# A two-layer FoX and GLA trunk: the sums of squares of three norms added up ahead of the product with ones

## The chip, the cores and the metric

The kernel runs on one core of one Trainium2 chip. The metric is the device time of one execution in microseconds (us), median of several runs. TensorE is called PE here, its weight loads PEld; VectorE is DVE, ScalarE ACT, GpSimd POOL, and SyncE, which issues most DMAs, SP.

## The reference, cut to what matters

A sequence of 1024 tokens of width 1024 passes two layers. Each has a token mixer (forgetting attention in layer 0, gated linear attention in layer 1) and a SwiGLU, and each of the four sub-layers is preceded by an RMS norm with shift and scale:

```python
def rms_norm(x, g):
    xf = x.astype(jnp.float32)
    y = xf * lax.rsqrt(jnp.mean(xf * xf, axis=-1, keepdims=True) + EPS)
    return (y * g.astype(jnp.float32)).astype(x.dtype)
...
    h = modulate(rms_norm(x, norm1_g[i]), sh1, sc1)
...
    x = x + g1[:, None, :] * y
    h = modulate(rms_norm(x, norm2_g[i]), sh2, sc2)
    x = x + g2[:, None, :] * swiglu(h, ffn_w_in[i], ffn_w_out[i])
```

The change concerns how the sum over the 1024 channels of `xf * xf` is formed in three of these norms.

## The kernel before, in words

Activations lie transposed: channels on the 128 partitions, in eight tiles of 128 channels, tokens along the free side. Tokens are worked in two halves of 512. Matrix products are made of three float32r products of a high and a low part (`mm3`, L241 to L243), with a pace that PE sets through most of the program.

A sub-layer ends in `last_chunk`. It projects the last four blocks of the inner dimension, for the first half of the tokens and then for the second. For each of the eight channel tiles m, DVE adds the scaled product to the residual stream (`x`, L1061), ACT squares the new tile (L577), and the object `SumSq` adds squares together, on POOL or DVE (L584). What it has not added up at the end are its *roots*. `rms_cols` (L524 to L534) then sums over partitions and roots at once: for each of four blocks of 128 tokens it multiplies every root, as the stationary operand, with a column of ones, and accumulates in one column of a PSUM tile `sp` (L529). DVE adds EPS to the mean (L532, tile `rs`), POOL raises it to the power -0.5 (L533), and four products (L541, tile `rb`) spread the result over all partitions, for DVE to multiply with.

In the first half there is one root (four products). In the second half `SumSq` has `late` = 7 (`LATE1`): the eighth square is not added to anything, and of the first seven there are three sums, so that there are four roots, v[0] (tiles 0 to 3), v[4] (tiles 4 and 5), v[6] and v[7], and sixteen products. This happens in three places: **place 1**, the norm ahead of the SwiGLU of layer 0 (tile `sp011`); **place 2**, the norm ahead of the gated linear attention (`sp101`); **place 3**, the norm ahead of the SwiGLU of layer 1 (`sp111`). The last norm has another form (`late` = 0) and isn't touched.

The products with ones are covered by other work on PE: at places 1 and 3 by the first tiles of the SwiGLU (`plain_tile`, tile `p`), which work on the first half of the tokens, at place 2 by the value projection of the first tokens (`gv_body`, tile `gv`). `issue_after` puts the products behind them in the order. Otherwise a scheduler orders each engine's instructions by a timeline of its own, so an edit may move others too. Each engine takes its instructions in that order.

At place 2 the two buffer slots named s39 and s40 hold four of the squares (v[3], v[4], v[5], v[7]). They are used next for the tiles `ad` (the running sum and two raw tiles of the second layer's modulation, and the mask that a DVE memset at L1567 fills). SP loads the raw tiles (L361), ACT scales them (L375, L377), POOL adds them (L379).

At places 1 and 3 POOL makes the sums of weight blocks (`op_sums`, L702 to L704) when their raw tiles `xv` have landed.

## Time and profile before

| | |
|---|---|
| median of 3 runs | 2429.87 us (2428.5 to 2430.59) |
| profiled execution, its own time | 2430.71 us |
| its span, first to last instruction | 2429.0 us |
| PE busy | 2375.2 us, 98% |
| DVE, ACT, POOL busy | 1689.5, 1192.6, 1164.0 us |
| mean granted clock of TensorE | 0.992 |

Times in a timeline are microseconds from the start of the span. A row gives the start, how long the instructions last, engine, line, operation, the tile written and those read, shapes, how many instructions are merged in the row, and in brackets how long the engine sat idle just before and what ended that. A float32 product appears as two passes (x2) of a weight load and a matmul. A matmul's end is modelled, and matmuls overlap, so the time that one takes from PE is read from the start of one to the start of the next. A table by windows gives for each stretch the engines' busy time, and the clock that TensorE was granted (1.00 is full speed).

### The profile page before, as it was taken

How to read it: one execution, taken by the hardware profiler on the slowest of the kernel's cores; microseconds unless marked ns; L12 is line 12 of the kernel's file. 1: busy time of each engine (PE TensorE's matmuls, PEld its weight loads, DVE VectorE, ACT ScalarE, POOL GpSimd, SP SyncE). 2: the span in 40 equal slices, each digit the busy share in tenths (PEclk: the TensorE clock that was granted, in tenths of full speed). 3: DMA queues.
4: the chain of work that ended last, by engine and by line, in shares of the span. 5: the costliest groups of instructions: out<-in, count | busy, mean ns of one | idle time of the engine just before them, and what ended most of it. 6: DMA issues, size and time to landing. Idle time of an engine off the chain costs nothing.

```text
span 2429.0 us, 36104 instructions
## 1 busy us (share of the span) xinstructions
PE 2375.2 (98%) x12338; PEld 2019.5 (83%) x12338; DVE 1689.5 (70%) x2845; ACT 1192.6 (49%) x2286; POOL 1164.0 (48%) x1015
## 2 busy tenths in 40 slices
PE   7999999999999999999999999999999999999998
PEld 6788888878888888888888798898888888888888
DVE  6578777676687777766788545436587767666787
ACT  4656556666544444445324756654343334345325
POOL 3333333333337878753363544552335656653362
PEclk9999999999999999999999999999999999999999
DMA  9233333123326555457665334444325434347664
GB/s 271 80 105 113 94 108 113 62 88 120 118 96 192 180 167 171 156 187 262 229 204 168 83 114 117 126 126 156 109 84 186 152 135 155 128 169 258 231 209 148
DMA packets 329503, 362.40 MB, mean 149 GB/s; under 512 B 24476, under 2 KB 252984, under 8 KB 329320
## 3 DMA queue, kind: packets, MB, share of 16 engines
q1 hardware_dynamic: 329128, 360.09, 46.2%
q8 instruction: 97, 1.59, 0.3%
q14 instruction: 86, 0.70, 0.1%
q10 hardware_dynamic: 192, 0.02, 0.0%
HBM read 269.78 MB, written 90.24 MB: 148 GB/s over the span
## 4 chain that ended last, share of the span: by engine, by line
PE 78%; DVE 6%; DMA 6%; ACT 3%; issue 2%; POOL 2%; SPq 2%; DVEq 0%; POOLq 0%; ACTq 0%
PE p_b L241 16%; PE p_b L243 16%; PE p_b L242 16%; PE o_b L968 2%; PE t_b L954 2%; SPq L361 1%; DMA ad_s<-in_ada_w_dram 1%; PE qk_b L241 1%; PE qk_b L242 1%; PE qk_b L243 1%; DMA ada_s<-in_ada_w_dram 1%; PE s_b L923 1%; PE s_b L924 1%; PE vps_b L241 1%; PE vps_b L242 1%
## 5 line engine op out<-in xcount | busy, mean ns | idle before, releaser
L164 DVE TENSOR_TENSOR o_s<-xv_s,o_s 128x512 fp32r<-128x512 f32 (+1 forms) x376 | 333.4, 890 | 82.3 <-ACT o_s L163 81.3
L163 ACT CAST o_s<-xv_s 128x512 fp32r<-128x512 f32 (+1 forms) x376 | 217.9, 586 | 319.5 <-PE p_b L243 250.8
L934 POOL TENSOR_SCALAR lp_s<-lp_s,st 128x128 f32<-128x128 f32 (+7 forms) x128 | 98.5, 775 | 291.1 <-DVE st L933 273.1
L242 PE MATMUL p_b<-B,o_s 128*128 128x512 f32 x608 | 237.8, 391 | 0.0
L243 PE MATMUL p_b<-B,o_s 128*128 128x512 f32 x608 | 237.2, 391 | 0.0
L241 PE MATMUL p_b<-B,o_s 128*128 128x512 f32 x608 | 236.6, 392 | 0.0
L702 POOL TENSOR_TENSOR ex_s<-xv_s,xv_s 128x512 f32<-128x512 f32 (+1 forms) x64 | 86.4, 1350 | 270.2 <-DMA xv_s<-in_ffn_w_in_dram 108.3
L241 PE MATMUL p_b<-T,o_s 128*128 128x512 f32 x480 | 186.7, 389 | 0.0
L242 PE MATMUL p_b<-T,o_s 128*128 128x512 f32 x480 | 186.7, 389 | 0.0
L243 PE MATMUL p_b<-T,o_s 128*128 128x512 f32 x480 | 180.7, 389 | 0.0
L932 ACT ACTIVATE lp_s<-lp_s,st 128x128 f32<-128x128 f32 (+7 forms) x128 | 99.3, 776 | 76.7 <-DVE st L928 73.9
L241 PEld LDWEIGHTS p_b<-B,o_s 128*128 128x128 f32 x608 | 115.0, 189 | 23.8
L243 PEld LDWEIGHTS p_b<-B,o_s 128*128 128x128 f32 x608 | 114.7, 189 | 24.0
L242 PEld LDWEIGHTS p_b<-B,o_s 128*128 128x128 f32 x608 | 114.9, 189 | 23.7
L1306 DVE TENSOR_TENSOR ex_s<-ex_s,p_b 128x512 f32<-128x512 f32 x140 | 93.6, 680 | 31.8 <-PE p_b L243 31.7
L704 POOL TENSOR_TENSOR xv_s<-ex_s,xv_s 128x512 f32<-128x512 f32 (+1 forms) x64 | 85.9, 1342 | 52.3 <-DVE o_s L164 49.7
L163 ACT CAST pt_s<-t_b 128x512 fp32r<-128x512 f32 (+1 forms) x160 | 79.9, 548 | 62.5 <-PE t_b L954 61.6
L243 PEld LDWEIGHTS p_b<-T,o_s 128*128 128x128 f32 x480 | 90.1, 188 | 18.8
L241 PEld LDWEIGHTS p_b<-T,o_s 128*128 128x128 f32 x480 | 90.1, 188 | 18.7
L242 PEld LDWEIGHTS p_b<-T,o_s 128*128 128x128 f32 x480 | 90.1, 188 | 18.6
L164 DVE TENSOR_TENSOR pt_s<-t_b,pt_s 128x512 fp32r<-128x512 f32 (+1 forms) x160 | 96.5, 631 | 11.4 <-ACT pt_s L163 10.8
L968 PE MATMUL o_b<-pt_s,v_s 128*128 128x256 f32 x512 | 95.6, 295 | 5.9 <-DVE pt_s L164 4.2
(1950 smaller groups left out, 7494.7 us busy)
## 6 DMA issues: line engine op xcount, KB each, us to landing
xv_s<-in_ffn_w_in_dram SPq DMA_DIRECT2D x176, 256.0 KB, 3.3
hid_B<-x SPq DMA_DIRECT2D x70, 512.0 KB, 2.8
ad_s<-in_ada_w_dram SPq DMA_DIRECT2D x384, 64.0 KB, 2.0
hid_T<-x SPq DMA_DIRECT2D x36, 512.0 KB, 2.8
xv_s<-in_ffn_w_out_dram SPq DMA_DIRECT2D x96, 192.0 KB, 5.1
ada_s<-in_ada_w_dram SPq DMA_DIRECT2D x128, 128.0 KB, 2.7
xv_s<-in_ffn_w_out_dram SPq DMA_DIRECT2D x40, 256.0 KB, 2.8
T2o<-hid_T SPq DMA_DIRECT2D x18, 512.0 KB, 9.0
```

The source lines that it names most:

```text
L163: nc.scalar.copy(hi, src)
L164: nc.vector.tensor_sub(lo, src, hi.bitcast(F32))
L241: nc.tensor.matmul(ps, ah, bh, start=start, stop=False)
L242: nc.tensor.matmul(ps, ah, bl, start=False, stop=False)
L243: nc.tensor.matmul(ps, al, bh, start=False, stop=stop)
L702: nc.gpsimd.tensor_add(s1, a21, a22)
L704: nc.gpsimd.tensor_sub(a11, s1, a11)
L932: nc.scalar.activation(lp, lp, AF.Exp, bias=mcur, scale=-1.0, accum_out=st[:, qi, 2:3])
L934: nc.gpsimd.tensor_scalar(lp, lp, st[:, qi, 3:4], 1.0, op0=ALU.mult, op1=ALU.mult)
L954: nc.tensor.transpose(tp[:, i, :], lps[qi][:, psl(2 * b + jj)], ident)
L968: nc.tensor.matmul(ops, lv, pts[b][:, hl, 2 * jj:2 * jj + 2, :], start=j == 0 and hl == 0, stop=False)
L1306: nc.vector.tensor_add(d, d if src is None else dest(G, src), ps)
```

## The change

The first seven squares are added up to one sum. Two additions on DVE come right behind the square of the seventh tile: v[4] += v[6], v[0] += v[4]. The roots of the second halves are then v[0] and v[7]: eight products with ones at each of the three places.

```diff
@@ -569,8 +569,7 @@
             self.late = late
-            self.roots = {0: [self.v[0]], 8: [self.v[0]], 7: [self.v[0], self.v[4], self.v[6], self.v[7]],
-                          5: [self.v[0], self.v[4], self.v[5], self.v[6], self.v[7]]}[self.late]
+            self.roots = [self.v[0], self.v[7]] if late == 7 else [self.v[0]]
 
@@ -583,6 +582,9 @@
                 d *= 2
+            if m == 6 and self.late == 7:
+                for i, j in ((4, 6), (0, 4)):
+                    nc.vector.tensor_add(v[i], v[i], v[j])
```

Lines behind the edit are numbered two higher in the changed kernel. On PE at place 1, before, the products `sp011` follow the last product of a SwiGLU tile (`p0`). In the slots' names, ss0_s31 holds v[0], s34 v[4], s32 v[6] and s33 v[7]; the four products of the first token block end this piece (a product with v[0] for it stands 27 rows earlier, and the other blocks follow with the same four).

```order
L241 MATMUL p0_b4_1_7658<-B2103_7112,o00001_s20_2_7452 128x512
L242 MATMUL p0_b4_1_7658<-B2103_7112,o00001_s20_2_7452 128x512
L243 MATMUL p0_b4_1_7658<-B2103_7112,o00001_s20_2_7452 128x512
L529 MATMUL sp011_b6_3_7485<-ones_74,ss0_s34_7104 128x1
L529 MATMUL sp011_b6_3_7485<-ones_74,ss0_s32_7102 128x1
L529 MATMUL sp011_b6_3_7485<-ones_74,ss0_s33_7103 128x1
L529 MATMUL sp011_b6_3_7485<-ones_74,ss0_s31_7101 128x1
```

On PE at place 1, after the change, the same rows read:

```order
L241 MATMUL p0_b4_1_7652<-B2103_7112,o00001_s20_2_7452 128x512
L242 MATMUL p0_b4_1_7652<-B2103_7112,o00001_s20_2_7452 128x512
L243 MATMUL p0_b4_1_7652<-B2103_7112,o00001_s20_2_7452 128x512
L529 MATMUL sp011_b6_3_7487<-ones_74,ss0_s31_7101 128x1
L529 MATMUL sp011_b6_3_7487<-ones_74,ss0_s33_7103 128x1
```

The eight products stand where fifteen stood, the sixteenth, which stood earlier, is gone, and the first of them now reads v[0], the sum that is finished last. Places 2 and 3 look the same.

On DVE at place 1 the last rows of the second half of the projection, before, up to the step that reads `sp011`:

```order
L1061 SCALAR_TENSOR_TENSOR x0_6_6208<-fo1461p_b2_15_7455,modc_168,x0_6_6208 128x512
L1061 SCALAR_TENSOR_TENSOR x0_7_6209<-fo1471p_b3_16_7470,modc_168,x0_7_6209 128x512
L584 TENSOR_TENSOR ss0_s34_7104<-ss0_s34_7104 128x512
L532 TENSOR_SCALAR rs011_7502<-sp011_b6_3_7485 128x4
L1162 SCALAR_TENSOR_TENSOR yb0_s31_7526<-x0_0_6202,amul_169,rb011_b7_4_7505 128x512
```

The same on DVE after the change:

```order
L1063 SCALAR_TENSOR_TENSOR x0_6_6208<-fo1461p_b2_15_7455,modc_168,x0_6_6208 128x512
L1063 SCALAR_TENSOR_TENSOR x0_7_6209<-fo1471p_b3_16_7472,modc_168,x0_7_6209 128x512
L583 TENSOR_TENSOR ss0_s34_7104<-ss0_s34_7104 128x512
L587 TENSOR_TENSOR ss0_s34_7104<-ss0_s34_7104,ss0_s32_7102 128x512
L587 TENSOR_TENSOR ss0_s31_7101<-ss0_s31_7101,ss0_s34_7104 128x512
L532 TENSOR_SCALAR rs011_7496<-sp011_b6_3_7487 128x4
```

The two additions stand behind the last one that was there, and nothing else moves; place 3 looks the same. At place 2 other work stands between. On DVE, before, from the last residual tile of the SwiGLU (`x0_7`) on; se0_s40 holds v[4], s38 v[6], s36 v[0], `w2t` is a small weight, `gvt00` the split of the first value tile, `ad_s40` the mask:

```order
L1061 SCALAR_TENSOR_TENSOR x0_7_6209<-f0e11871p_b5_16_12886,modc_168,x0_7_6209 128x512
L584 TENSOR_TENSOR se0_s40_12503<-se0_s40_12503 128x512
L164 TENSOR_TENSOR w2t_12977<-w2raw_s18_93_12974,w2t_12977 16x512 x2
L164 TENSOR_TENSOR gvt00_s53_1_13074<-gv00_b0_1_13012,gvt00_s53_1_13074 128x512
L1567 MEMSET ad_s40_12966 128x512
L1568 MEMSET ad_s40_12966 128x4
L532 TENSOR_SCALAR rs101_12918<-sp101_b3_1_12901 128x4
```

On DVE at place 2 after the change:

```order
L1063 SCALAR_TENSOR_TENSOR x0_7_6209<-f0e11871p_b5_16_12882,modc_168,x0_7_6209 128x512
L583 TENSOR_TENSOR se0_s40_12497<-se0_s40_12497 128x512
L164 TENSOR_TENSOR w2t_12965<-w2raw_s18_93_12962,w2t_12965 16x512 x2
L587 TENSOR_TENSOR se0_s40_12497<-se0_s40_12497,se0_s38_12495 128x512
L164 TENSOR_TENSOR gvt00_s53_1_13062<-gv00_b0_1_13000,gvt00_s53_1_13062 128x512
L587 TENSOR_TENSOR se0_s36_12494<-se0_s36_12494,se0_s40_12497 128x512
L1569 MEMSET ad_s40_12954 128x512
L1570 MEMSET ad_s40_12954 128x4
L532 TENSOR_SCALAR rs101_12906<-sp101_b3_1_12897 128x4
```

The additions come in behind `w2t` and behind `gvt00`. ACT behind place 2, before, from the first modulation tiles (`ad`) on; `te0` and `h1` are the normed second half, `gvt01` the split of the second value tile:

```order
L375 ACTIVATE ad_s39_12965<-ad_s39_12965,cblk_97 128x512
L377 ACTIVATE ad_s40_12966<-ad_s40_12966,cblk_97 128x512
L377 ACTIVATE ad_s39_12965<-ad_s39_12965,cblk_97 128x512
L555 ACTIVATE h1h0_12676<-te0_s31_12504,modc_168 128x512
L560 ACTIVATE te0_s31_12504<-te0_s31_12504,modc_168,amul_169 128x512
L555 ACTIVATE h1h2_12680<-te0_s32_12505,modc_168 128x512
L561 CAST h1h1_12678<-te0_s31_12504 128x512
L377 ACTIVATE ad_s40_12966<-ad_s40_12966,cblk_97 128x512
L163 CAST gvt01_s25_2_13134<-gv01_b1_2_13077 128x512
```

ACT there after the change:

```order
L377 ACTIVATE ad_s40_12954<-ad_s40_12954,cblk_97 128x512
L375 ACTIVATE ad_s39_12953<-ad_s39_12953,cblk_97 128x512
L555 ACTIVATE h1h0_12670<-te0_s31_12498,modc_168 128x512
L377 ACTIVATE ad_s39_12953<-ad_s39_12953,cblk_97 128x512
L560 ACTIVATE te0_s31_12498<-te0_s31_12498,modc_168,amul_169 128x512
L555 ACTIVATE h1h2_12674<-te0_s32_12499,modc_168 128x512
L163 CAST gvt01_s25_2_13122<-gv01_b1_2_13065 128x512
```

The cast of `gvt01` stands two rows earlier, ahead of a cast and of an `ad` tile, and `h1h0` comes ahead of the third `ad` tile. SP issues the four DMAs of the first `ad_s40` tile ahead of those of `ad_s39`, where two of each alternated. On PE one product `z` of the gate stands three `gv` products later.

## Prediction

> **What bounds the kernel now.** I read the page first, then the chain of work that ended last, then the timelines of the three places, and a table of windows for the granted clock. The page says where the time is:

> ```profile
> span 2429.0 us, 36104 instructions
> PE 2375.2 (98%) x12338; PEld 2019.5 (83%) x12338; DVE 1689.5 (70%) x2845; ACT 1192.6 (49%) x2286; POOL 1164.0 (48%) x1015
> ```

> PE is busy for 98% of the span, so what PE is spared counts, and what PE must newly wait for counts as well. The chain that ended last holds the products with ones at all three places:

> ```profile
> 676.42 3.50 PE sp_b L529 x30
> ...
> 1327.35 3.08 PE sp_b L529 x26
> ...
> 1772.05 3.45 PE sp_b L529 x30
> ```

> They are on the path, about 3.5 us at each place. Place 1 on PE, as a timeline:

> ```profile
> 669.66 0.28 PE L529 MATMUL sp_b<-ones,ss_s 128*128 128x1 f32 x2
> ...
> 676.03 0.39 PE L243 MATMUL p_b<-B,o_s 128*128 128x512 f32 x1
> 676.26 3.66 PE L529 MATMUL sp_b<-ones,ss_s 128*128 128x1 f32 x30
> 679.77 0.77 PE L241 MATMUL p_b<-B,o_s 128*128 128x512 f32 x1
> ...
> 683.72 0.40 PE L243 MATMUL p_b<-B,o_s 128*128 128x512 f32 x1
> 683.95 1.06 PE L541 MATMUL rb_b<-ident,rs 128*128 128x128 f32 x8
> ```

> Three things are to be seen. Fifteen products take 30 passes from 676.26 to 679.77, 0.117 us a pass, 0.23 us a product; the sixteenth stands alone at 669.66 and costs as much. A product of the SwiGLU starts 0.23 us behind the one before. And the twelve such products from 679.77 to 683.95 took 4.18 us where 12 x 0.23 is 2.7. The table by windows says why, and shows the same elsewhere (the windows are the stretches in which the clock records change, all 3.41 us long and on one grid through the whole trace):

> ```profile
> 675.83:679.25 3.42, 3.42 (x31) 1.00 0.45 178
> 679.25:682.66 3.41, 3.41 (x11) 0.50 0.03 7
> 1324.37:1327.78 3.41, 2.73 (x24) 1.00 1.00 300
> 1327.78:1331.19 3.41, 3.41 (x32) 1.00 0.80 265
> 1331.19:1334.61 3.42, 3.42 (x19) 0.50 0.67 179
> 1341.43:1344.85 3.42, 1.31 (x6) 1.00 0.35 88
> 1344.85:1348.26 3.41, 3.41 (x8) 0.50 0.30 73
> 1771.51:1774.93 3.42, 3.42 (x31) 1.00 0.46 183
> 1774.93:1778.34 3.41, 3.41 (x11) 0.50 0.00 0
> ```

> The third column is the granted clock. After a window filled with products of one column, and after one in which PE mostly waited (1.31 us busy of 3.42), the clock is 0.50 for a window. Eight products started in such a window (1344.85), 0.43 us each, where 15 would have: about 1.5 us lost. A window with a wait of 0.7 us in it (1324.37) had no such effect. I call PE **thinly used** when it waits or makes one-column products; somewhere between 1.3 and 2.27 us of that in one window halves the next one. I take 2.1 us, near the rows that did halve.

> **What the change removes.** Eight products with ones at each place, 16 passes of 0.117 us: 1.87 us on PE, 5.6 us for the three. That would be the gain, 0.23%, if nothing waited.

> **What it adds: two additions on DVE ahead of the first product.** The products are in order on PE, and the first of them now needs v[0], finished last. Behind it waits all of PE. So the question is when the two additions end. At place 1, DVE and POOL:

> ```profile
> 674.48 0.68 DVE L584 TENSOR_TENSOR ss_s<-ss_s 128x512 f32<-128x512 f32 x1
> ```

> ```profile
> 674.70 1.61 POOL L702 TENSOR_TENSOR ex_s<-xv_s,xv_s 128x512 f32<-128x512 f32 x1 [14.24 <-DMA xv_s<-in_ffn_w_in_dram]
> 676.39 1.27 POOL L703 TENSOR_TENSOR xv_s<-xv_s 128x512 f32<-128x512 f32 x1
> ```

> The last addition that exists ends at 675.16, and DVE is then free. Two more at 0.68 us each, with 0.05 us between them, would end at 676.6. But POOL's addition at 674.70 takes 1.61 us where the next takes 1.27: it waited for DVE's. That the two engines take turns, and DVE waits as well, is shown by the first half at place 3, where DVE's additions last 1.16 and 1.11 us beside one on POOL:

> ```profile
> 1742.92 1.16 DVE L584 TENSOR_TENSOR ss_s<-ss_s 128x512 f32<-128x512 f32 x1
> 1744.11 1.11 DVE L584 TENSOR_TENSOR ss_s<-ss_s,ss_s 128x512 f32<-128x512 f32 x1
> ```

> ```profile
> 1743.49 1.19 POOL L209 TENSOR_TENSOR wo_768l_s<-wo_s,wo_768h_s 128x256 fp32r<-128x256 f32 x1
> ```

> POOL's ends at 1744.68, 0.6 us behind the end of DVE's first (1744.08), and DVE's second ends at 1745.22, 0.55 us behind POOL's. So at place 1 I let them take turns: POOL's L702 ends at 676.31 as now; the first new addition ends 0.55 us later, 676.86; POOL's L703, pending since 676.39, ends 1.15 us behind that (as L702 does behind 675.16), 678.01; the second new addition ends at 678.56. PE, 0.23 us ahead without the early product, comes to the products at 676.03 and waits till 678.6. Sixteen passes take 1.87 us, to 680.5, against 679.77 now: **0.7 us later**. Thin use lasts from 676.03 to 680.5, 4.5 us, and so one half-clock window follows as now; where a window's edge lies early in the stretch (I put it at one run in three), a second follows, 1.6 us more.

> Place 3 has the same work, with POOL's additions a little later:

> ```profile
> 1770.11 0.68 DVE L584 TENSOR_TENSOR ss_s<-ss_s 128x512 f32<-128x512 f32 x1
> ```

> ```profile
> 1771.06 1.28 POOL L702 TENSOR_TENSOR ex_s<-xv_s,xv_s 128x512 f32<-128x512 f32 x1 [14.98 <-DMA xv_s<-in_ffn_w_in_dram]
> ```

> ```profile
> 1771.89 3.61 PE L529 MATMUL sp_b<-ones,ss_s 128*128 128x1 f32 x30
> 1775.36 0.77 PE L241 MATMUL p_b<-B,o_s 128*128 128x512 f32 x1
> ```

> The first new addition runs from 1770.84 to 1771.52 and is ahead of POOL; POOL's follows, to 1772.67; the second ends at 1773.22. Products from 1773.28 to 1775.15, against 1775.36: **0.2 us earlier**. Thin use lasts 3.5 us, as now.

> At place 2 POOL is idle, but DVE isn't. DVE, then PE:

> ```profile
> 1326.62 0.67 DVE L584 TENSOR_TENSOR se_s<-se_s 128x512 f32<-128x512 f32 x1
> 1327.22 1.38 DVE L164 TENSOR_TENSOR w2t<-w2raw_s,w2t 16x512 fp32r<-16x512 f32 x2
> 1328.63 0.69 DVE L164 TENSOR_TENSOR gvt_s<-gv_b,gvt_s 128x512 fp32r<-128x512 f32 x1
> ...
> 1344.11 0.69 DVE L164 TENSOR_TENSOR gvt_s<-gv_b,gvt_s 128x512 fp32r<-128x512 f32 x1 [0.85 <-ACT gvt_s L163]
> ```

> ```profile
> 1327.35 3.51 PE L529 MATMUL sp_b<-ones,se_s 128*128 128x1 f32 x30 [0.68 <-DVE se_s L584]
> 1330.72 0.36 PE L241 MATMUL gv_b<-wv_0h_s,h1h 128*128 128x256 f32 x1
> ...
> 1335.16 1.05 PE L541 MATMUL rb_b<-ident,rs 128*128 128x128 f32 x8
> ...
> 1342.35 0.39 PE L1592 MATMUL aps_b<-h1l,aw_s 128*128 128x512 f32 x1
> 1344.85 0.79 PE L241 MATMUL gr_b<-h1h,w_h_s 128*128 128x512 f32 x1 [2.11 <-DVE gvt_s L164]
> ```

> PE already waits here for v[4] (0.68 us). By the new order DVE does both `w2t` splits (to 1328.60), an addition (to 1329.2), `gvt00` (to 1329.9) and the second addition, to 1330.5. The products then run from 1330.55 to 1332.4, against 1330.72: 1.7 us later, and `rb` with them, 1.5 us more if a second half-clock window follows, which is likelier here (thin use for 5.9 us). But behind `rb` PE has 7.4 us of work (1335.16 to 1342.58) and then waits 2.27 us for `gvt01`. That wait gets shorter: the cast of `gvt01` stands two rows earlier on ACT, DVE waited 0.85 us for it, and so `gr` follows `rb` by 8.85 us, not 9.7. PE waits 1.4 us there in place of 2.27, under what halves the clock, and the half window from 1344.85 (1.6 us) goes. `gr` ends 1.7 - 0.85 - 1.6 = 0.8 us earlier, or with the second window 0.7 us later. I take **nothing** for place 2.

> The additions' own time on DVE, 6 x 0.68 us, lies where DVE was idle (4.8 us at places 1 and 3 ahead of L532). Moved `ad` DMAs start some 2 us later, but the running sum is due only after 1364. Nothing else moves.

> **The sum.** 0.7 + 0 - 0.2 = 0.5 us more. On the profiled execution, 2430.71 us with 1.7 us around its span, this gives 2431.2; it ran 0.84 us above the median, so for a median I say 2430.4 us.

> **The rivals.** *The turns are missed*, because a DMA of `xv` lands later and POOL comes behind both additions. Then the products start at 676.7 and 1772.3, end 1.2 us earlier than now at both places: -2.4 us in all. If thin use (2.7 us) then halves no clock there, 1.45 us more at each: -5.3, 2424.5 us. For it: landing times vary (POOL came 0.22 us behind DVE's start at place 1, 0.95 at place 3). Against: POOL must come 1 us later at place 1. One in twelve.

> *The clock stays full at places 1 and 3* though the turns are as I say: 0.7 - 1.45 and -0.2 - 1.45, -2.4 us in all, 2427.5 us. Against it are the rows: 3.5 us of thin use halved it. For it: the place's edge on the grid is by chance, and the bound of 2.1 us isn't sharp. One in six. [...]

> *The delay at place 2 is not absorbed.* The late products free v[7]'s slot late, SP's `ad` loads start after them, and ACT, in order, waits for the third `ad` tile ahead of `te0` as now, so that `gvt01` keeps its 9.7 us behind `rb`, PE its wait, and the clock its half window. Then place 2 costs 1.7 us, 3.2 with a second window; with the two windows at place 1 as well (2.3) and -0.2, 5.3 us in all: 2435.2 us, slower than before. It decides from the point where the `ad` tile lands more than 0.85 us behind `h1h0`. Against it: `h1h0` now stands ahead of that tile. One in six, half of it with only one window at place 1 or 2, some 2433.

> That the scheduler undid the edit can't be: its rows are in the order above.

> **How the numbers follow.** Forecast as above, with -1.5 to +2.8 us by windows, 0.58; turns missed 0.08; clock full 0.17; not absorbed 0.17. The range takes in the second and most of the last, less and plus 1 us by which runs differ: 2426.5 to 2434.5. A measurement can tell about 0.2%, 4.9 us, from no change. Beyond that lie, on the fast side, half of the first rival: 0.05; on the slow side half of the last: 0.09; within: 0.86.

> **What would show it.** The products with ones as 16 passes at each place; PE idle ahead of them, released by DVE's second addition, 2.6 us at place 1, 1.6 at place 3, 4 at place 2; POOL's L703 between the two additions at place 1; a shorter wait at `gr`. I am wrong if DVE makes both additions in a row beside POOL, if the clock is full behind the products, or if `gr` waits as long as before.

## The result, and the profile after

The changed kernel takes 2435.38 us (median of 20 runs, 2432.1 to 2442.91), the kernel before 2429.47 us (20 runs beside them, 2424.64 to 2430.89). The ratio is 1.0028, 95% interval 1.0022 to 1.0034: by this ratio slower by 6.8 us (5.3 to 8.3); the two medians lie 5.9 us apart. The forecast was no change, 2430.4 us, with 2434.5 us as the upper end.

The page of the changed kernel (its profiled execution took 2435.12 us):

```profile
span 2433.4 us, 36022 instructions
...
PE 2372.8 (98%) x12290; PEld 2017.9 (83%) x12290; DVE 1708.6 (70%) x2851; ACT 1196.4 (49%) x2286; POOL 1165.7 (48%) x1015
```

PE has 48 passes less (24 products), as meant. It is busy 2.4 us less, and yet the span is longer. Place 1 as a timeline, all engines, of which these rows matter:

```profile
671.13 1.86 POOL L704 TENSOR_TENSOR ex_s<-xv_s,xv_s 128x512 f32<-128x512 f32 x1 [13.99 <-DMA xv_s<-in_ffn_w_in_dram]
671.16 0.67 DVE L583 TENSOR_TENSOR ss_s<-ss_s 128x512 f32<-128x512 f32 x1
671.94 3.27 DVE L587 TENSOR_TENSOR ss_s<-ss_s,ss_s 128x512 f32<-128x512 f32 x2
673.07 1.59 POOL L705 TENSOR_TENSOR xv_s<-xv_s 128x512 f32<-128x512 f32 x1
...
675.36 3.52 PE L529 MATMUL sp_b<-ones,ss_s 128*128 128x1 f32 x16 [2.51 <-DVE ss_s L587]
678.75 0.77 PE L241 MATMUL p_b<-B,o_s 128*128 128x512 f32 x1
...
683.20 1.05 PE L541 MATMUL rb_b<-ident,rs 128*128 128x128 f32 x8
```

PE stands still for 2.51 us until DVE's second addition ends. The two additions last 3.27 us where 1.36 would do, with POOL's second one between them. Then come 16 passes, which last from 675.36 to 678.75, 3.4 us: nearly as long as the 30 passes of before (3.5 us). The windows on the clock's grid say why (columns: window, its length, PE's busy time and matmuls, granted clock, DMA share and GB/s):

```profile
671.98:675.40 3.42, 0.91 (x5) 1.00 0.61 241
675.40:678.81 3.41, 3.41 (x17) 0.50 0.00 0
678.81:682.22 3.41, 3.41 (x9) 0.50 0.01 2
682.22:685.64 3.42, 3.42 (x20) 1.00 0.02 5
```

Behind the window with the wait in it (PE busy for 0.91 us of 3.42) the next has a clock of 0.50; the products with ones run in it, 16 passes in 3.4 us, and fill it to the end; and the one behind it has 0.50 as well. Two half-clock windows, where the kernel before had one. Place 3, as a timeline:

```profile
1772.18 1.90 POOL L704 TENSOR_TENSOR ex_s<-xv_s,xv_s 128x512 f32<-128x512 f32 x1 [13.96 <-DMA xv_s<-in_ffn_w_in_dram]
1772.26 0.68 DVE L583 TENSOR_TENSOR ss_s<-ss_s 128x512 f32<-128x512 f32 x1
1773.04 3.26 DVE L587 TENSOR_TENSOR ss_s<-ss_s,ss_s 128x512 f32<-128x512 f32 x2
...
1776.44 2.22 PE L529 MATMUL sp_b<-ones,ss_s 128*128 128x1 f32 x16 [2.50 <-DVE ss_s L587]
```

The same picture: a wait of 2.50 us, and by the clock records two half windows, from 1777.9 to 1784.7. Place 2, as a timeline:

```profile
1324.30 0.67 DVE L583 TENSOR_TENSOR se_s<-se_s 128x512 f32<-128x512 f32 x1
1324.89 1.38 DVE L164 TENSOR_TENSOR w2t<-w2raw_s,w2t 16x512 fp32r<-16x512 f32 x2
1326.31 0.69 DVE L587 TENSOR_TENSOR se_s<-se_s,se_s 128x512 f32<-128x512 f32 x1
1326.92 0.68 DVE L164 TENSOR_TENSOR gvt_s<-gv_b,gvt_s 128x512 fp32r<-128x512 f32 x1
1327.52 0.68 DVE L587 TENSOR_TENSOR se_s<-se_s,se_s 128x512 f32<-128x512 f32 x1
1328.35 3.55 PE L529 MATMUL sp_b<-ones,se_s 128*128 128x1 f32 x16 [3.65 <-DVE se_s L587]
```

and its windows:

```profile
1323.93:1327.34 3.41, 0.77 (x7) 1.00 0.79 276
1327.34:1330.75 3.41, 2.40 (x12) 0.50 0.76 217
1330.75:1334.17 3.42, 3.42 (x17) 0.50 0.24 69
1334.17:1337.58 3.41, 3.41 (x18) 0.50 0.19 51
```

A wait of 3.65 us behind `w2t` and `gvt00`, and three half windows in a row. PE's waits, summed over the whole execution by the view of waits (total, number, longest), show both new ones:

```profile
PE sp_b L529 <- DVE ss_s L587: 5.0, 2, 2.5
...
PE sp_b L529 <- DVE se_s L587: 3.6, 1, 3.6
```

To see where the time went I measured the same stretches in every profiled execution: at places 1 and 3 from the first SwiGLU product (tile `p`) to `rb`, at place 2 from the first value product `gv` to the gate product `z`, all as starts on PE.

| stretch, us | before | after | difference |
|---|---|---|---|
| place 1, `p` to `rb` | 14.74 | 17.31 | +2.57 |
| place 2, `gv` to `z` | 35.50 | 37.28 | +1.78 |
| place 3, `p` to `rb` | 14.73 | 16.82 | +2.09 |

Together 6.4 us, close to the measured 6.8. The rest of the two traces does not count against the change: ahead of place 1, where the kernels are the same, after is 3.3 us earlier (before's execution had two half windows at 300 us that after's had not), and the attention of layer 1, from the first product of `kdt` to the last tile of its projection, took 377.24 us in before and 378.95 in after; but it took 378.7 to 381.0 in the five other kernels below that keep four roots at place 2, so that before's execution was the odd one.

One execution of each kernel is a small sample of half windows. The granted clock of every execution is a larger one: its mean is 0.9910 over the 20 executions of the changed kernel, and 0.9930 to 0.9932 in the four groups of executions of the kernel before that ran beside the experiments below (13 to 34 each). A half window (3.41 us at 0.50) takes 0.0007 off the mean clock of an execution of 2430 us, so by this estimate the changed kernel has some three half windows more than before, worth about 1.7 us each.

### The profile page after: what moved, and what is told of

Its sections match the earlier page's. It is cut to its first block, busy times and chain, and to the rows that moved or that the text cites. A ratio compares the mean times of both kernels' runs of the same rounds, so it can differ in the third digit from the quotient of the medians.

```text
span 2433.4 us, 36022 instructions
## 1 busy us (share of the span) xinstructions
PE 2372.8 (98%) x12290; PEld 2017.9 (83%) x12290; DVE 1708.6 (70%) x2851; ACT 1196.4 (49%) x2286; POOL 1165.7 (48%) x1015
## 5 line engine op out<-in xcount | busy, mean ns | idle before, releaser
L164 DVE TENSOR_TENSOR o_s<-xv_s,o_s 128x512 fp32r<-128x512 f32 (+1 forms) x376 | 338.4, 903 | 81.7 <-ACT o_s L163 80.7
L163 ACT CAST o_s<-xv_s 128x512 fp32r<-128x512 f32 (+1 forms) x376 | 218.9, 588 | 322.7 <-PE p_b L243 254.1
L243 PE MATMUL p_b<-B,o_s 128*128 128x512 f32 x608 | 237.6, 391 | 0.0
L241 PE MATMUL p_b<-B,o_s 128*128 128x512 f32 x608 | 237.1, 393 | 0.0
L241 PE MATMUL p_b<-T,o_s 128*128 128x512 f32 x480 | 186.7, 389 | 0.0
L243 PE MATMUL p_b<-T,o_s 128*128 128x512 f32 x480 | 180.7, 389 | 0.0
L243 PEld LDWEIGHTS p_b<-B,o_s 128*128 128x128 f32 x608 | 115.1, 189 | 24.1
L241 PEld LDWEIGHTS p_b<-B,o_s 128*128 128x128 f32 x608 | 115.1, 189 | 23.8
L163 ACT CAST pt_s<-t_b 128x512 fp32r<-128x512 f32 (+1 forms) x160 | 80.1, 549 | 62.0 <-PE t_b L956 61.1
L243 PEld LDWEIGHTS p_b<-T,o_s 128*128 128x128 f32 x480 | 90.1, 188 | 18.7
L241 PEld LDWEIGHTS p_b<-T,o_s 128*128 128x128 f32 x480 | 90.1, 188 | 18.6
L164 DVE TENSOR_TENSOR pt_s<-t_b,pt_s 128x512 fp32r<-128x512 f32 (+1 forms) x160 | 96.5, 631 | 11.4 <-ACT pt_s L163 10.9
```

The costliest lines, as they stand in the source:

```text
L163: nc.scalar.copy(hi, src)
L164: nc.vector.tensor_sub(lo, src, hi.bitcast(F32))
L241: nc.tensor.matmul(ps, ah, bh, start=start, stop=False)
L243: nc.tensor.matmul(ps, al, bh, start=False, stop=stop)
```

## The experiments

Theory A: PE's wait for the late additions is the loss, with the half-clock windows that it brings. Its rivals: the additions cost by themselves (B), place 2 alone is the loss (C), the eight products left halve the clock even without a wait (D), and later E, that POOL's additions delay other work by as much as PE is spared. Ratios are against the kernel before, run beside each; one thousandth is 2.4 us.

| run | ratio (95%) | us | place 1, 3, us | place 2, us |
|---|---|---|---|---|
| changed kernel | 1.0028 (1.0022 to 1.0034) | +6.8 | 17.31, 16.82 | 37.28 |
| e1: place 2 only | 1.0020 (1.0011 to 1.0029) | +4.9 | (14.58, 13.14) | 37.79 |
| e2: places 1 and 3 only | 1.0028 (1.0017 to 1.0040) | +6.8 | 15.69, 17.27 | (34.83) |
| e3: fewer products, no additions, two sums left out | 0.9956 (0.9944 to 0.9969) | -10.7 | 11.35, 11.35 | 30.92 |
| e4: additions, all products | 1.0002 (0.9993 to 1.0011) | +0.5 | (14.70, 16.23) | (35.50) |
| b1: change, products later | 0.9998 (0.9987 to 1.0009) | -0.5 | 12.77, 12.77 | 39.63 |
| b2: before, products later | 0.9999 (0.9988 to 1.0009) | -0.2 | 15.07, 14.88 | (32.89) |
| b3: place 2, additions first | 1.0009 (1.0000 to 1.0018) | +2.2 | (16.33, 16.21) | 33.90 |
| b5: places 1 and 3, products later | 0.9979 (0.9967 to 0.9991) | -5.1 | 12.77, 12.76 | (35.04) |
| c1: additions on POOL | 1.0007 (0.9998 to 1.0016) | +1.7 | 15.50, 16.73 | 32.22 |
| c2: places 1 and 3, wait filled | 0.9995 (0.9986 to 1.0004) | -1.2 | 14.11, 15.37 | (35.16) |
| d1: b1 with POOL at place 2 | 0.9971 (0.9960 to 0.9982) | -7.1 | 12.78, 12.82 | 32.38 |
| d2: b1 with b3 | 0.9973 (0.9961 to 0.9985) | -6.6 | 12.77, 12.76 | 32.67 |

The stretches are of one execution each, those in brackets of places where PE has the same products as before; they scatter, since a half-clock window more or less moves them by 1.5 us (e4: 14.70 us with one at place 1, 16.23 with two at place 3). Places 1 and 3 with four roots and no wait ran ten times in these traces (before, e1, e4, b2, b3); two half windows in a row came at three of them (e4 place 3, both of b3), one at six, none at one. In b1, b2, b5, d1 and d2 the stretch to `rb` holds six SwiGLU products more, 1.4 us.

**One part of the change alone.** `at` is the name that `last_chunk` is called with, "fo", "f0e" and "go" for places 1, 2 and 3:

```diff
-            self.roots = [self.v[0], self.v[7]] if late == 7 else [self.v[0]]
+            self.sum7 = late == 7 and at in ("f0e",)
+            self.roots = ([self.v[0], self.v[7]] if self.sum7 else
+                          [self.v[0], self.v[4], self.v[6], self.v[7]] if late == 7 else [self.v[0]])
...
-            if m == 6 and self.late == 7:
+            if m == 6 and self.sum7:
```

> The change at place 2 alone; places 1 and 3 keep four roots. Theory A (the loss is PE's wait for the second addition, and the half-clock windows that the wait brings): place 2 cost 1.8 us from the first value product to the product z in the changed kernel's trace, and 1.7 us more came behind it, at a wait ahead of the GLA states; if both belong to place 2, +1.8 to +3.5 us against before, ratio 1.0007 to 1.0014, with PE waiting 3.6 us ahead of the products and two or more half windows there. Rival B (the additions' load on DVE and what they displace costs, wherever they are): a third of the loss, +2 us, and it comes back in the run that only adds. Rival C (place 2 is the whole loss, since its delay moves the running sum and all of GLA): +6 us.

> The change at places 1 and 3 alone; place 2 keeps four roots. Theory A: +2.6 us at place 1 and +2.1 us at place 3, as the changed kernel's trace has it from the first SwiGLU product to the product rb, so about +4.7 us against before, ratio 1.0019, with a wait of 2.5 us and two half windows at each. Rival C (place 2 is the whole loss): within 1 us of before. If by chance the grid of windows cuts the stretch so that one half window does, Theory A gives 1.5 us less at that place.

Both parts cost. Each came out above what A gave, though its interval holds it (2.7 to 7.1 and 4.1 to 9.7 us), and the two add up to 11.7 us where the whole change costs 6.8; the intervals just about meet, and what makes the difference is not settled. C is out, since places 1 and 3 cost without it. e2 brought the same wait in two ways. The windows of e2 at place 1, where most of the wait and nearly all the passes lay in one window:

```profile
672.00:675.41 3.41, 2.73 (x13) 1.00 0.97 353
675.41:678.82 3.41, 1.58 (x15) 1.00 0.15 59
678.82:682.24 3.42, 3.42 (x11) 0.51 0.01 2
682.24:685.65 3.41, 3.41 (x20) 1.00 0.02 5
```

The passes ran at full rate (2.0 us), one half window followed, and the place cost 0.95 us, near the 0.7 that the prediction has for just this case. At place 3 of e2 two windows followed, and it cost 2.5 us.

**The two halves of the change apart.** First the eight products without the additions, then the additions without the saving:

```diff
-            if m == 6 and self.late == 7:
-                for i, j in ((4, 6), (0, 4)):
-                    nc.vector.tensor_add(v[i], v[i], v[j])
```

> Eight products with ones at each place, and no addition: the sums v[4] and v[6] are left out of the norm, so that the numbers are not the reference's, and PE has nothing new to wait for. Theory A: PE saves 8 x 2 x 0.11 us at each place, 5.4 us in all; 1.8 us of one-column products with no wait ahead of them halves no clock, which gives 1.4 us more at places 1 and 3 and 1.6 us at place 2: -8 to -10 us, ratio 0.9960 to 0.9967. Rival D (the one-column products halve the clock however few they are, and the wait has no part in it): the windows behind the three places stay half; the products run in part at half rate, and the gain is 3 to 5 us, ratio 0.998 to 0.999. Rival B says the same as A here.

```diff
-            self.roots = [self.v[0], self.v[7]] if late == 7 else [self.v[0]]
+            self.roots = [self.v[0], self.v[4], self.v[6], self.v[7]] if late == 7 else [self.v[0]]
...
-                for i, j in ((4, 6), (0, 4)):
-                    nc.vector.tensor_add(v[i], v[i], v[j])
+                for o, i, j in ((5, 4, 6), (3, 0, 5)):
+                    nc.vector.tensor_add(v[o], v[i], v[j])
```

> The two additions at each place are made, into tiles that nothing reads (v[5] = v[4] + v[6], v[3] = v[0] + v[5]), and the four roots with their sixteen products stay as before. Theory A: DVE and POOL take turns as in the changed kernel (POOL's first addition 1.9 us), but PE doesn't wait for it: within 1 us of before, ratio 0.9996 to 1.0004, half windows as before. Rival B (the load of the additions): +4 to +6 us, as in the changed kernel.

The products alone are worth 10.7 us (7.5 to 13.6), half of it passes (48 x 0.117 us is 5.6) and the rest windows: e3 has no half window at places 1 and 3, and `rb` follows the passes at full pace. PE in e3, place 1, as a timeline:

```profile
674.08 1.62 PE L529 MATMUL sp_b<-ones,ss_s 128*128 128x1 f32 x14
678.38 1.05 PE L541 MATMUL rb_b<-ident,rs 128*128 128x128 f32 x8
```

So D is out: the passes of four roots (30 in a row in before and e4), without a wait, had a half-clock window behind them at nine of ten places, the sixteen of two roots, without a wait, at none of ten (1 and 3 in e3, b1, b5, d1, d2). The additions alone cost nothing that can be measured, though in e4's timeline DVE and POOL take the same turns as in the changed kernel; PE, with the additions off its path, has no idle time in front of its row:

```profile
671.19 1.79 POOL L704 TENSOR_TENSOR ex_s<-xv_s,xv_s 128x512 f32<-128x512 f32 x1 [14.06 <-DMA xv_s<-in_ffn_w_in_dram]
671.94 3.27 DVE L587 TENSOR_TENSOR ss_s<-ss_s,ss_s 128x512 f32<-128x512 f32 x2
...
672.92 3.40 PE L529 MATMUL sp_b<-ones,ss_s 128*128 128x1 f32 x30
```

B is out too. The loss is neither of the halves, it is that one waits for the other.

**The wait covered by real work.** At places 1 and 3 the products with ones stand twelve SwiGLU products later:

```diff
-    GK = (2, 6)
+    GK = (6, 8)
```

b1 is the change with this line, b2 the kernel before with it, b5 is e2 with it.

> The change, and at places 1 and 3 the products with ones stand twelve SwiGLU products later on PE, and rb six products behind them. Theory A (PE's wait and the half-clock windows that it brings are the loss): in the changed kernel the second addition ended 9.3 us behind the first SwiGLU product, and PE now comes to the products 9.8 us behind it, so that it doesn't wait; the sixteen passes take 1.5 us at full clock as in the run without additions, and the clock stays full. Each of the two places then gives 3.4 us against before, 6.8 us, less what place 2 costs (1.8 to 4.9 us by the runs so far): -2 to -5 us, ratio 0.998 to 0.999, and some 9 us less than the changed kernel. Rival B (the additions, their turns with POOL and the displaced work cost by themselves): +5 to +7 us as in the changed kernel. Rival D (the products halve the clock without a wait): 2.8 us more than A.

> The kernel before with the same shift of the products with ones and of rb at places 1 and 3, and nothing else: the control for the run above. Theory A: no wait there before, none now; 32 passes still fill most of a window and halve the next, so within 1 us of before, ratio 0.9996 to 1.0004. If rb's later place delays the second half's norm, +0.5 to +2 us. If the later place by itself brought the gain of the run above, it would show here as -2 us or more.

> The change at places 1 and 3 alone, with the products with ones later there, and four roots at place 2. Theory A: 3.4 us at each of the two places and nothing at place 2: -7 us against before, ratio 0.9971 (0.9963 to 0.9980). Rival B (the additions cost by themselves): +4 to +7 us as the run with places 1 and 3 alone. Rival D: -4 us.

PE in b1, place 1, as a timeline; no idle time in front, and 16 passes at full rate:

```profile
678.26 1.90 PE L529 MATMUL sp_b<-ones,ss_s 128*128 128x1 f32 x16
681.51 1.16 PE L541 MATMUL rb_b<-ident,rs 128*128 128x128 f32 x8
```

DVE's two additions lasted 3.30 us there, and nobody waited for them. The control b2 shows that the later place is worth nothing to four roots. With the change at places 1 and 3 it is worth 12 us: 1.0028 for e2, 0.9979 for b5. b1 gained less than A said, -0.5 where -2 to -5 was expected; its places 1 and 3 came out as in b5, and its place 2 took 39.63 us in the profiled execution, with four half windows in it; place 2 alone had cost 4.9 us in e1, about what b1 falls short of b5.

**Place 2.** The `w2t` splits and the splits of the value tiles are put behind the second addition:

```diff
+                add_ins.append(last_ins())
...
+        with tc.issue_after(add_ins[-1]):
             split(w2t[r0:r0 + 16, 0, :], w2t[r0:r0 + 16, 1, :], w2raw[r0:r0 + 16, :])
```

> The change at place 2 alone, with the two additions on DVE right behind the sum of tiles 4 and 5, ahead of the w2t splits and of gvt00. Theory A: v[0] is finished 2.0 us earlier than in the run with place 2 alone, PE's wait ahead of the products falls from 3.6 us or more to about 2, and with it the third half window goes: 2 to 4 us less than that run, 0 to +3 us against before, ratio 1.0000 to 1.0012. Rival C (the delayed modulation loads and what follows from them are the loss at place 2): as that run, +5 us, ratio 1.002.

PE's wait fell from 4.0 us in e1 to 2.29 us and the cost from 4.9 to 2.2 us, as A had it. The two intervals overlap, so this difference alone is not clear of noise; but the +5 us (1.002) of C lie outside b3's interval, if only just. In no kernel was the later running sum felt: from `z` to the first product of `kdt` all fourteen traces agree within 0.2 us (31.3 us). So the wait, with its windows, is the likeliest cost at place 2 as well; no run filled it there, as the next one does at places 1 and 3.

**The wait's length and the clock, told apart.** Eleven products that nobody needs, ahead of the products with ones, give PE work for as long as it would wait; the change stands at places 1 and 3 alone:

```diff
+                if after and k == GK[0] == after[0][0]:
+                    fl_ = pin([P, HALF], F32, f"fl{l}")
+                    for _ in range(11):
+                        nc.tensor.matmul(fl_, w.hi[:, 0, :], hi(b["B11"][0]), start=True, stop=True)
```

> The change at places 1 and 3 alone, with eleven products of 512 columns more on PE ahead of the products with ones, into a tile that nothing reads: 11 x 0.227 = 2.5 us of idle work where PE waited 2.5 us. The time that PE loses to the second addition is the same; only the clock's part goes. Theory A with the clock (a wait costs its length and the half-clock windows that it brings): the windows behind the products are full, and each place costs 2.5 - 3.4 = -0.9 us against before: -1.8 us, ratio 0.9993, and 8 us less than the run with places 1 and 3 alone. Theory A without the clock (the wait's length is the loss): as that run, +4 to +7 us, ratio 1.002 to 1.003.

PE in c2, place 1, as a timeline (the scheduler set the eleven among the SwiGLU products ahead, as five, one and five; the first row has the last five):

```profile
675.39 1.30 PE L1332 MATMUL fl_b<-B,o_s 128*128 128x512 f32 x5
...
677.87 1.92 PE L529 MATMUL sp_b<-ones,ss_s 128*128 128x1 f32 x16
...
682.48 1.05 PE L541 MATMUL rb_b<-ident,rs 128*128 128x128 f32 x8
```

PE comes to the products 9.50 us behind the first `p`, as it did after its wait in e2 (9.47), and loses the same 2.5 us to the additions. But the kernel takes 8 us less than e2 (0.9995 against 1.0028; 4 to 12 us), and with the time of the wait filled there are fewer half windows, none at place 1 and one at place 3. The mean granted clock of the executions goes the same way, 0.9915 in e2 (6) and 0.9944 in c2 (10): by the same estimate four half windows less. A without the clock is out: the clock's part of the loss at places 1 and 3 (8 us, 4 to 12) is about as large as the 5.0 us of waits, or larger.

**The additions on an engine that idles.** POOL makes `v[4] += v[5]` and `v[0] += v[4]` behind the sixth square, and DVE only `v[0] += v[6]`:

```diff
-                (nc.gpsimd if d == 1 and m < 4 else nc.vector).tensor_add(v[m - 2 * d + 1], v[m - 2 * d + 1], v[m - d + 1])
+                (nc.gpsimd if d == 1 and m < (6 if self.late == 7 else 4) else nc.vector).tensor_add(
+                    v[m - 2 * d + 1], v[m - 2 * d + 1], v[m - d + 1])
...
-            if m == 6 and self.late == 7:
-                for i, j in ((4, 6), (0, 4)):
-                    nc.vector.tensor_add(v[i], v[i], v[j])
+            if m in (5, 6) and self.late == 7:
+                (nc.gpsimd if m == 5 else nc.vector).tensor_add(v[0], v[0], v[4 if m == 5 else 6])
```

> The same sums and the same eight products at all three places, but by another way: behind the sixth square POOL, which idles there, adds v[4] += v[5] and v[0] += v[4], and only v[0] += v[6] is left to DVE, behind the seventh square, where the kernel before has v[4] += v[5]; at place 2 the w2t splits come behind it on DVE. Theory A (PE's wait for late additions is the loss, not the additions): v[0] is finished no later than v[4] was before, PE waits 0.7 us or less at place 2 and not at all at places 1 and 3, and as in the run without additions each of places 1 and 3 gives 3.4 us and place 2 2 to 4.6 us: -8 to -11 us against before, ratio 0.9955 to 0.9967. Rival B (the additions cost wherever they are made): +5 us. If POOL's 1.3 us each make its weight sums late at places 1 and 3, 1 to 2 us less gain.

A clear miss: +1.7 us. DVE and POOL in c1, place 1, as a timeline:

```profile
671.17 1.28 DVE L164 TENSOR_TENSOR o_s<-xv_s,o_s 128x512 fp32r<-128x512 f32 x2
671.33 2.27 POOL L583 TENSOR_TENSOR ss_s<-ss_s 128x512 f32<-128x512 f32 x1 [10.34 <-ACT ss_s L576]
672.37 3.48 DVE L1172 SCALAR_TENSOR_TENSOR B<-ya_s,modc,B 128x512 fp32r<-128x512 f32 x2
673.68 1.62 POOL L586 TENSOR_TENSOR ss_s<-ss_s,ss_s 128x512 f32<-128x512 f32 x1
...
675.77 0.74 DVE L1063 SCALAR_TENSOR_TENSOR x<-fo1461p_b,modc,x 128x512 f32<-128x512 f32 x1
```

and the same step of DVE in the kernel before:

```profile
671.84 1.41 DVE L1170 SCALAR_TENSOR_TENSOR B<-ya_s,modc,B 128x512 fp32r<-128x512 f32 x2
673.16 0.74 DVE L1061 SCALAR_TENSOR_TENSOR x<-fo1461p_b,modc,x 128x512 f32<-128x512 f32 x1
```

Two steps of DVE took 3.48 us in place of 1.41, each ending 0.55 us behind one of POOL's two additions (these end at 673.60 and 675.30), and everything behind them on DVE was 2.07 us late: the seventh tile stands 6.02 us behind the first `p`, not 3.95. So `v[0]` was late all the same, and PE waited 2.3 us at places 1 and 3. POOL was idle, but not free for this. At place 2 it did better: PE doesn't wait for the products with ones, and the stretch takes 32.22 us, where kernels with four roots there took 32.89 to 35.50.

**The pieces that helped, together.** d1 is the change with the line above (6, 8), and c1's additions at place 2 alone; d2 is b1 with the lines of b3:

```diff
+            self.pool = late == 7 and at == "f0e"
...
-            if m == 6 and self.late == 7:
+            if self.pool and m in (5, 6):
+                (nc.gpsimd if m == 5 else nc.vector).tensor_add(v[0], v[0], v[4 if m == 5 else 6])
+                add_ins.append(last_ins())
+            elif m == 6 and self.late == 7:
```

> The pieces that helped, together: the change at places 1 and 3 with its products later on PE (there the run with places 1 and 3 alone gave -5.1 us), and at place 2 v[4] += v[5] and v[0] += v[4] on POOL behind the sixth square, v[0] += v[6] on DVE ahead of the w2t splits. Theory A (what PE waits for, and the half-clock windows that the wait brings): in the run with POOL's additions the stretch from the first value product to z took 32.2 us at place 2, where kernels with four roots there took 32.9 to 35.5; so 0 to 3 us are added: -5 to -8 us against before, ratio 0.9967 to 0.9979. Rival E (POOL's additions delay what POOL and DVE do for the first half's tiles, as at places 1 and 3, by as much as PE is spared): no better than -5 us, and perhaps -2 us.

> As the run beside it, but at place 2 the change as it is with the two additions ahead of the w2t splits and of gvt00 on DVE; alone that measured +2.2 us against before (0 to +4.4). Theory A: PE waits some 2.3 us ahead of the products there, so -5.1 + 2.2 = -3 us, ratio 0.9988 (0.998 to 0.9995), 3 to 5 us more than the run beside it. Rival E: less than the run beside it, since POOL is left alone.

d1 takes 2424.08 us (median of 7 runs; before, beside it, 2431.51 of 13), 7.1 us less than the kernel before (4.4 to 9.7) and, by the ratios, some 14 less than the changed kernel. It beats both. d2 came out better than expected, 6.6 us below before, and can't be told from d1: in its trace PE waits 0.5 us ahead of the products at place 2, not 2.3, as DVE's second addition ends 8.9 us behind the first `gv`, in b3 10.7; why DVE is earlier there stays open. So POOL's additions at place 2 bring little over DVE's in the right order. E isn't settled for that place (PE waits 3.0 us for POOL's tiles `h1l` there in d1, 2.1 in d2); at places 1 and 3 c1 bears it out.

## Why the prediction was wrong, step by step

- **What the change removes: the passes right, their worth too small.** 16 passes went at each place. But 5.6 us "if nothing waited" counts the passes alone; without a wait e3 gained 10.7 us, since the half windows went too.
- **Turns and wait at place 1: right.** The additions took 3.27 us in turn with POOL, as worked out, and PE waited 2.51 us where 2.6 was forecast.
- **"One half-clock window follows as now", a second in one run of three: this is the step that failed.** Of the four places with such a wait (places 1 and 3 in the changed kernel and in e2), three had two windows; with the waits of 2.3 us in c1 it is four of six. Place 1 cost 2.57 us, not 0.7; where only one followed (e2), it cost 0.95. The base was not firm either: one window was what the single trace of before had, and four roots without a wait had two at three places of ten. Over all places the sum, as I took it, had no half window more; by the mean clock of all executions there were some three more, about 5 us, most of the miss of 6.3. The bound of 2.1 us of thin use in a window was taken from windows at full clock, and for those with SwiGLU products the estimate from the counts of the last section agrees (2.0 to 2.2 us). For a window that is half already the same estimate gives far less (0.8 to 1.1 us), and at place 1 of the changed kernel the products with ones, having waited, fell into just such a window, by where the grid's edge lay; there they also lasted twice as long (16 passes in 3.4 us, 1.76 in b1). I had counted them at full rate.
- **Place 3, a wait of 1.6 us and a gain of 0.2: wrong in size.** POOL's `xv` landed ahead of DVE's addition, at 5.2 us behind the first `p` where before had 6.2, so the turns of place 1 came here too: 2.50 us of wait, two windows, +2.09.
- **Place 2, nothing: wrong.** The wait (3.65, forecast 4) and the shorter wait at `gr` (1.6, forecast 1.4, and no half window behind it) came as written; but three half windows came in a row, the first of them (from 1327.34) already within the wait, where the sum had one and allowed for two. The loss of 1.78 us lies there; alone, in e1, place 2 cost 4.9 us (2.7 to 7.1). The third rival named this place and a price near it (1.7 to 3.2), but by another mechanism, the late `ad` tile, of which the trace shows nothing.
- **The other rivals.** The turns weren't missed, and the clock didn't stay full.

The three stretches together, 2.57 + 1.78 + 2.09 = 6.4 us, lie within the interval of the measured loss.

## What to carry to other kernels

An addition that saves PE work is worth it only if its result is there when PE comes to it; a wait in front of short products cost its length here (2.5 us at places 1 and 3) and then the clock, 0.50 in the window behind it, and in one more where short products fell into that window (places 1 and 3 of the changed kernel). Give PE other work in front (b5: twelve products moved turned +6.8 us into -5.1) before counting the saving. An engine without work is free for a helper only if it doesn't hold up the busy one, as POOL held up DVE in c1 (3.48 us for 1.41).

## What the runs showed of the hardware

| windows in order | columns and clock |
|---|---|
| before, place 1 | 972 (full), 3,292 (half), then full |
| after, place 1 | 1,591 (full), 84 (half), 3,920 (half), then full |
| e2, place 1 | 14 (full), 3,392 (half), then full |
| after, place 3 | 14 (full), 3,161 (half), 3,590 (half), then full |
| e3, place 1 | 5,131 and 6,466 (full), full |

The last row but one shows how little decides it: 0.6 us of passes in a half window left 3,161 columns, and the next was half too, where 3,292 and 3,392 were followed by full ones. Waiting and one-column products came to the same here: at 1341.43 in before PE was busy for 1.31 us of 3.42, at 1771.51 for all of the 3.42 us, with 31 passes, and behind both the clock was 0.50.

**A pass of one column cost 0.11 us at full clock and 0.21 at half** (16 passes in 1.76 us in b1 and in 3.4 us in the changed kernel, both at place 1), so its cost went with the clock.

**In c1 DVE and POOL took turns though they worked on different tiles.** At place 1 POOL's additions (1.28 us at the shortest in before) took 2.27 and 1.62, and two steps of DVE 3.48 us in place of 1.41.
